# First S5 layer of a four-layer trunk: GpSimd's operator work in tied groups, zeros and counts moved, fewer unread products, another order for sines and tanh

## The chip, the cores and the metric

The kernel runs on one core of one Trainium2 chip. The metric is the device time of one execution in microseconds, lower is better. Before the change it is 2245.62 us (median of three runs, 2242.55 to 2246.93). A core has five engines that work side by side, each in the order of its own queue: PE (TensorE, matmul), VectorE (DVE), ScalarE (ACT), GpSimd (POOL) and SyncE (SP, which here only starts transfers). They wait for each other through semaphores.

## The reference, cut to what matters

The model is a trunk of four layers on 512 tokens of width 1024; layers 0 and 3 mix with S5, layer 1 with gated linear attention, layer 2 with differential attention, and each is followed by a gated feed-forward block. The change touches the first S5 layer (layer 0). There 64 groups of 16 channels each have a diagonal complex state of 64 entries:

```python
dt = jnp.exp(log_dt)[:, None]
ab_mag, ab_ang = jnp.exp(lr * dt), li * dt              # the pole of each state
bb_re = f_re[..., None] * br - f_im[..., None] * bi     # input operator, f from the pole
bb_im = f_re[..., None] * bi + f_im[..., None] * br
# s[t] = ab * s[t-1] + bb @ u[t]   (complex), by an associative scan
y = einsum('bcgp,ghp->bcgh', s_re, cr) - einsum('bcgp,ghp->bcgh', s_im, ci)
z = gelu(y + d_skip * h)
a, b = split(z @ w_glu)                                 # 1024 x 2048 weights
mix = a * sigmoid(b)
```

## The kernel before, in words

Four successive tokens form one step of the scan, so a scan has 128 steps. The 64 groups are 32 pairs on the 128 partitions, and the pairs are worked off in eight blocks of four (`kk` = 0 to 7), each 512 columns wide. For every block the kernel needs operators: `X` (input, with powers 0 to 3 of the pole) and `Q` (output, powers 0 to 4). These are made for two blocks at once, for `h` = 0 to 3, by `cross` (L1228), which multiplies by the powers and adds: three elementwise operations a time (L1239, L1240, L1241). `s5_x` (L1255) gives `X` and three functions: `pre` (the gain, and power 0), `one` (real part of powers 1 to 3) and `two` (imaginary part). `X[0]` is made on VectorE, `X[1]`, `X[2]` and `X[3]` on GpSimd, all of `Q` on VectorE.

The rotation of each state is taken out of the scan, so that the scan runs on real decays (`r4`, L1221), and the phases come from `s5_phases_first` (L1187): PE multiplies `counts` (numbers 0 to 127 on block-selecting rows) with the phase rows `frow`; ScalarE rounds twice ("rough"); PE subtracts ("angle"); VectorE clips; ScalarE takes two sines.

`s5_first` (L1763) sets all this up, and `s5_pipe` (L1542) runs the iterations `kk` = 0 to 9. In iteration `kk`, in this order: `states(kk)` on VectorE (L1593 to L1598; the first four read PE's products `V` from PSUM, the last two have both inputs in SBUF), `outputs(kk - 1)` on PE (`y`, L1628 and L1630) with the gelu on ScalarE (L1632), `up(kk + 2)` and `products(kk + 1)` (V), `turned(kk - 1)` (PE `zp`, ScalarE `zT`), two scans (L1602) and four turn products (L1615, L1611) on VectorE, `rest(kk - 1)` on VectorE (L1653, reads PSUM), and matmuls of the following projection (`glu`, L1666). Hooks of `s5_first` insert operators, phases and transfers at named places. From L1675 (`hand_all`) on, the order on every engine is the program's order; ahead of it a scheduler picks the order, within the limits that `issue_after` sets.

Other pieces that the steps touch:
- The maps `mops` (input to output within a step) go through DRAM: `s5_map` (L1355) adds on VectorE, copies on ScalarE, stores on SP's queue and loads with eight DMAs, four on SP's and four on GpSimd's queue.
- `rps` (L1352) are products of `Q` with the padded `B` (`bp`); PE has them at the start of iterations 2, 4 and 6.
- `zero_off` (L1316) writes zeros into the off-diagonal halves of operator tiles, on ScalarE by copies of zeros out of the identity.
- `warmed(12)` (L1338) is twelve fp32 products of the identity with itself that nobody reads; in the trace they are 24 matmuls.
- Small PSUM tiles are taken in turn from two banks (`tp`), so PE's next transpose waits for the copy of the last but one.
- `s5_glu` (L2022) follows: tanh of four accumulators (`gate`, L2034), which frees their banks, and the product with the other half of the weights, whose tiles are cast on ScalarE (L420) and whose low parts are made on VectorE (L428).

## Time and profile before

| | |
|---|---|
| median of three runs | 2245.62 us |
| the profiled execution's own time | 2241.62 us |
| its span | 2239.9 us |
| TensorE's granted clock, mean | 0.998 |
| busy: PE, VectorE, ScalarE, GpSimd | 97%, 73%, 51%, 15% |
| first S5 layer up to its last `glu` matmul | 0 to 143.9 us |

The profile is one execution recorded by the hardware. A row of a timeline gives the start, the duration, the engine, the line of the kernel, the operation with its output and inputs and their shapes, and how many were merged (x4). What stands in square brackets is how long the engine had been idle before it and what ended that. Neighbouring instructions on one engine overlap a little, so durations add up to more than the elapsed time; the distance from start to start is what counts. The granted clock (PEclk) is 1.00 at full speed and 0.50 at half.

### The profile page before, as it was taken

Reading aid. Unit: us, or ns where it says so; the run is one execution under the profiler, and the core shown is the slowest. Engines: PE = TensorE matmul, PEld = TensorE weight load, DVE = VectorE, ACT = ScalarE, POOL = GpSimd, SP = SyncE. Lnnn points to the kernel's source line nnn. Section 1 sums busy time; section 2 is a strip of 40 time slices with the busy share of each in tenths; the row PEclk is TensorE's granted clock in tenths of the full one; section 3 lists DMA queues with packets and bytes.
Section 4 is the critical chain, followed back from the end, with each engine's and each line's share of the span. In section 5 each row is a group of like instructions: output and inputs, shape, how many; then the busy total and the mean of one; then the engine's idle time right before and its main releaser. Section 6 shows DMA issues by size and latency. Waiting matters only on the chain.

```text
span 2239.9 us, 38438 instructions
## 1 busy us (share of the span) xinstructions
PE 2171.3 (97%) x15415; PEld 1967.9 (88%) x15415; DVE 1635.7 (73%) x2495; ACT 1137.5 (51%) x1827; POOL 337.6 (15%) x447
## 2 busy tenths in 40 slices
PE   6999999999999999999999999999999999999998
PEld 5888979999988899999988888999999888989997
DVE  9965878786877598776745676977766965957675
ACT  8534635444655365564435676644544334635343
POOL 5301141431211010100002221101000001101000
PEclk9999999999999999999999999999999999999999
DMA  4256666774863667765337465985632646766632
GB/s 90 62 175 168 159 167 174 175 183 129 206 158 95 169 162 198 180 170 141 104 128 155 100 151 139 231 223 132 180 95 56 161 142 158 191 166 166 165 76 75
DMA packets 309180, 333.62 MB, mean 149 GB/s; under 512 B 70477, under 2 KB 253033, under 8 KB 308874
## 3 DMA queue, kind: packets, MB, share of 16 engines
q1 hardware_dynamic: 238970, 238.93, 35.3%
q0 software_dynamic: 70032, 92.23, 22.2%
q8 instruction: 121, 1.98, 0.4%
q14 instruction: 57, 0.47, 0.1%
HBM read 297.16 MB, written 18.75 MB: 141 GB/s over the span
## 4 chain that ended last, share of the span: by engine, by line
PE 80%; DVE 10%; ACT 4%; issue 3%; DMA 1%; SPq 1%; POOL 0%; DVEq 0%; POOLq 0%; ACTq 0%
PE a L594 20%; PE acc L448 11%; PE acc L450 11%; PE acc L449 11%; PE c L594 10%; PE d L594 5%; DVE whl L428 2%; PE y L1630 2%; PE acc L1666 2%; ACT whl L420 1%; PE op L2607 1%; PE s L2574 1%; PE tp L117 1%; PE V L1588 1%; PE acc L2662 1%
## 5 line engine op out<-in xcount | busy, mean ns | idle before, releaser
L428 DVE TENSOR_TENSOR whl<-wst,whl 128x1024 fp32r<-128x1024 f32 x260 | 317.0, 1224 | 220.7 <-ACT whl L420 219.7
L594 PE MATMUL a<-side,whl 128*128 128x256 f32 x3240 | 391.8, 277 | 6.6 <-DVE whl L428 6.3
L420 ACT CAST whl<-wst 128x1024 fp32r<-128x1024 f32 x260 | 272.0, 1051 | 244.9 <-PE acc L450 155.8
L594 PEld LDWEIGHTS a<-side,whl 128*128 128x128 f32 x3240 | 378.3, 188 | 8.9 <-DVE whl L428 7.4
L448 PE MATMUL acc<-whl,act 128*128 128x512 f32 x704 | 276.1, 392 | 1.6 <-DVE g L768 1.6
L449 PE MATMUL acc<-whl,act 128*128 128x512 f32 x704 | 274.6, 390 | 0.0
L450 PE MATMUL acc<-whl,act 128*128 128x512 f32 x704 | 274.5, 390 | 0.0
L594 PE MATMUL c<-side,whl 128*128 128x256 f32 x2160 | 260.9, 277 | 3.8 <-DVE whl L428 3.8
L594 PEld LDWEIGHTS c<-side,whl 128*128 128x128 f32 x2160 | 252.6, 188 | 4.7 <-DVE whl L428 4.6
L428 DVE TENSOR_TENSOR whl<-slot,whl 128x1024 fp32r<-128x1024 f32 x105 | 127.8, 1222 | 60.6 <-ACT whl L420 60.5
L448 PEld LDWEIGHTS acc<-whl,act 128*128 128x128 f32 x704 | 132.2, 188 | 30.1 <-DVE g L768 2.2
L450 PEld LDWEIGHTS acc<-whl,act 128*128 128x128 f32 x704 | 132.2, 188 | 27.7
L449 PEld LDWEIGHTS acc<-whl,act 128*128 128x128 f32 x704 | 132.3, 188 | 26.2
L420 ACT CAST whl<-slot 128x1024 fp32r<-128x1024 f32 x105 | 109.9, 1052 | 86.3 <-PE acc L450 46.3
L594 PE MATMUL d<-sides,whl 128*128 128x256 f32 x1080 | 132.3, 278 | 2.5 <-ACT whl L420 2.5
L594 PE MATMUL a<-sides,whl 128*128 128x256 f32 x1080 | 132.4, 279 | 1.9 <-DVE whl L428 1.2
L594 PEld LDWEIGHTS d<-sides,whl 128*128 128x128 f32 x1080 | 127.9, 188 | 3.3 <-ACT whl L420 3.3
L594 PEld LDWEIGHTS a<-sides,whl 128*128 128x128 f32 x1080 | 128.0, 188 | 3.2 <-DVE whl L428 1.4
L428 DVE TENSOR_TENSOR whl<-halves,whl 128x1024 fp32r<-128x1024 f32 x87 | 105.9, 1222 | 31.8 <-ACT whl L420 31.6
L420 ACT CAST whl<-halves 128x1024 fp32r<-128x1024 f32 x87 | 91.0, 1052 | 71.5 <-DVE halves L817 27.2
L759 POOL DMA_DIRECT2D wst<-in_ffn_w_gate_up_dram x44 | 57.1, 1299 | 449.2 <-DMA wst<-in_ffn_w_gate_up_dram 174.0
L865 ACT CAST act<-r 128x512 fp32r<-128x512 f32 (+1 forms) x110 | 66.1, 643 | 106.9 <-DVE r L846 85.7
(506 smaller groups left out, 4039.1 us busy)
## 6 DMA issues: line engine op xcount, KB each, us to landing
wst<-in_ffn_w_gate_up_dram SPq DMA_DIRECT2D x88, 512.0 KB, 4.7
wst<-in_ffn_w_down_dram SPq DMA_DIRECT2D x88, 512.0 KB, 4.6
slot<-in_ffn_w_gate_up_dram SPq DMA_DIRECT2D x69, 512.0 KB, 6.6
wst<-in_ffn_w_gate_up_dram POOLq DMA_DIRECT2D x44, 512.0 KB, 6.1
halves<-in_ffn_w_gate_up_dram SPq DMA_DIRECT2D x42, 512.0 KB, 7.0
wst<-in_s_w_glu_dram SPq DMA_DIRECT2D x32, 512.0 KB, 5.0
wst<-in_diff_w_qkv_dram SPq DMA_DIRECT2D x24, 512.0 KB, 4.3
slot<-in_ffn_w_gate_up_dram POOLq DMA_DIRECT2D x18, 512.0 KB, 9.4
```

The source lines that it names most:

```text
L117: tr.nc.tensor.transpose(p[:, j], h[:, j * P : (j + 1) * P], tr.ident[:])
L420: self.last["high"] = self.nc.scalar.copy(hl[:, 0], w[:])
L428: self.last["low"] = self.nc.vector.tensor_tensor(hl[:, 1], w[:], hl[:, 0].bitcast(F32), op=ALU.subtract)
L448: mm(out, lh, rh, start=first, stop=False)
L449: mm(out, lh, rl, start=False, stop=False)
L450: self.last["mm"] = mm(out, ll, rh, start=False, stop=last)
L594: mm(o, *two, start=first and not (j or k or n), stop=k == 3 and n == 2, skip_group_check=True,)
L759: nc.gpsimd.dma_start(w[:], left.quarter(*plus, b), accum_op=ALU.add)
L865: self.last["act high"] = nc.scalar.copy(dst[:, 0, j], src[:, j])
L1588: mm(V[kk][z][:, bs(b)], inm[:, z, bs(b)], U[:, bs(b)], start=True, stop=True)
L1630: mm(yb[:, b], q[:, j, b], om[:, j // 2, bs(b)], start=False, stop=j == 3)
L1666: mm(accs[t][:], zT[:, m // 2, kk, t * P : (t + 1) * P], hl[:, m % 2, kk % 2], start=kk == 0 and m == 0, stop=kk == KT - 1 and m == 2,)
```

## The change

- **Counts**: eight scaled copies on ScalarE instead of two products on VectorE.
- **Decays**: the copy on ScalarE leaves out the first column of each block; that column is zeroed once per buffer (`s5_no_decay`), in the first S5 on VectorE ahead of everything, in the second S5 (three buffers) on GpSimd. Before, GpSimd zeroed it after every copy.
- **Zeros of the maps**: `mops[0]` on VectorE ahead of everything, `mops[1]` on ScalarE at the end of iteration 0; before, both on ScalarE at the start.
- **Unread products**: `warmed(5)` instead of `warmed(12)`.
- **Sines**: ahead of the loop, clip and sines of block 0 come before the rough step of block 1.
- **GpSimd's X**: `pre`, `one` and `two` no longer run in one go. A group can begin with a copy of one column from a VectorE result into a place of `X` that `two` overwrites later, so that GpSimd waits for that result. `X[1]` (pre, one) waits for the end of `Q[0]`, and its `two` for the second turn product of iteration 0; `X[2]` (pre, one) waits for the end of `Q[1]`, `two` for the second turn product of iteration 2; `X[3]` (pre) waits for the end of `Q[2]`, its `one` and `two` for the second turn product of iteration 4. Before, `X[1]` began after the fourth root of the norm, and `X[2]` and `X[3]` stood at the turns of iterations 1 and 3 without such a wait.
- **Tanh**: in the first half of the first S5's gated projection, casts and low parts from the second weight block on are ordered behind the last tanh and the last low part before them.

```diff
@@ -1162,10 +1162,8 @@
         v.tensor_tensor(sel[:], self.ident[:, 4:8], self.ident[:, 8:12], op=ALU.add)
         self.counts = cp.tile([P, 2, 4, P], F32R, name="counts")
         for z, y in enumerate((self.ident[:, 0:4], sel[:])):
-            v.tensor_tensor(
-                self.counts[:, z], y.unsqueeze(2).broadcast_to([P, 4, P]),
-                self.mrow[:].unsqueeze(1).broadcast_to([P, 4, P]), op=ALU.mult,
-            )
+            for j in range(4):
+                nc.scalar.mul(self.counts[:, z, j], self.mrow[:], y[:, j : j + 1])
         self.nident = cp.tile([P, P], F32R, name="nident")
         nc.gpsimd.tensor_scalar_mul(self.nident[:], self.ident[:], -1.0)
         self.mmagic = cp.tile([P, 1], F32, name="mmagic")
@@ -1222,8 +1220,11 @@
         r = r4.rearrange("p (b m) -> p b m", m=P)
         c = L * NB + 4 * kk
-        self.nc.scalar.copy(r, self.k5["r4"][:, c : c + 4].unsqueeze(2).broadcast_to([P, 4, P]))
-        self.nc.gpsimd.memset(r[:, :, 0:1], 0.0)
+        self.nc.scalar.copy(r[:, :, 1:], self.k5["r4"][:, c : c + 4].unsqueeze(2).broadcast_to([P, 4, P - 1]))
+
+    def s5_no_decay(self, r4, eng):
+
+        eng.memset(r4.rearrange("p (b m) -> p b m", m=P)[:, :, 0:1], 0.0)
     def cross(self, eng, pool, L, b0, nb, s0, ns, out, a, b, op, w):
@@ -1553,6 +1554,7 @@
             q = self.wp.tile([P, 4, 4, P], F32, tag="whl", name="prods", bufs=5)
             nc.gpsimd.memset(q[:, :, :, 0:1], 0.0)
             hold.append((m, q))
+        self.turned_out = lambda kk: hold[kk % 2][1][:, 1, 3, 127:]
         wg = self.i["s5_w_glu"][L]
         stage, hls = {}, {}
         accs = []
@@ -1767,12 +1769,17 @@
         zT = zpool.tile([P, 2, KT, SEQ], F32R, name="zT")
         self.edge(zpool, 32)
         with self.tc.tile_pool(name="s5_0", bufs=1) as p:
+            r4 = {}
             scr, more = (self.hp.tile([P, 4096], F32, tag="hT", name=f"scr{z}") for z in range(2))
             oms = [more[:, 1024 * z : 1024 * z + 1024].rearrange("p (a b) -> p a b", a=2) for z in range(2)]
             mops = [more[:, 2048 + 1024 * z : 3072 + 1024 * z] for z in range(2)]
             bp = p.tile([P, 2, 256], F32, name="bpad")
             rs = p.tile([P, 2, 112], F32, name="rsb")
             inm = [p.tile([P, 2, 512], F32, name=f"inm{z}") for z in range(2)]
+            self.zero_off(mops[0].unsqueeze(1), 64)
+            for n in range(2):
+                r4[n] = p.tile([P, 512], F32, tag="r4", name="r4", bufs=2)
+                self.s5_no_decay(r4[n][:], nc.vector)
             self.s5_small(p)
             for t in range(NT):
                 nc.sync.dma_start(xin[:, t], i["x"][0].rearrange("(p t) c -> p t c", t=NT)[:, t])
@@ -1783,35 +1790,35 @@
                 nc.sync.dma_start(gain[g * 64 : (g + 1) * 64], src[g].partition_broadcast(64))
             raw = {0: self.s5_loads(p, 0, 0, 8, 2)}
             raw[1] = self.s5_loads(p, 0, 8, 8, 2)
-            X, Q, ph, r4 = {}, {}, {}, {}
-
-            def new_x(h):
-                X[h] = self.s5_x(nc.gpsimd if h else nc.vector, p, 0, 8 * h, 8, raw[h][0], 2, gain)
-                for f in X[h][1:] if h else X[h][1:2]:
-                    f()
+            X, Q, ph = {}, {}, {}
+
+            def new_x(h, *parts, behind=None):
+
+                if 0 in parts:
+                    X[h] = self.s5_x(nc.gpsimd if h else nc.vector, p, 0, 8 * h, 8, raw[h][0], 2, gain)
+                if behind is not None:
+                    nc.gpsimd.tensor_copy(X[h][0][:, 1, 7, 3, 15:], behind)
+                for n in parts:
+                    X[h][1 + n]()
             def new_q(h):
                 Q[h] = self.s5_q(nc.vector, p, 0, 8 * h, 8, 2)
                 Q[h][1](self.s5_qt(raw[h][1]))
-            rounded, *rows = self.s5_rows_of_phases(p)
-            for y in inm:
+            for y in inm + oms:
                 self.zero_off(y, 64, nc.scalar)
             self.zero_off(bp[:], 16, nc.scalar)
             nc.gpsimd.memset(rs[:, :, :48], 0.0)
-            for z in range(2):
-                self.zero_off(oms[z], 64, nc.scalar)
-                self.zero_off(mops[z].unsqueeze(1), 64, nc.scalar)
+            rounded, *rows = self.s5_rows_of_phases(p)
             with self.tc.issue_after(self.last_power.ins):
-                new_x(0)
-                X[0][2]()
+                new_x(0, 0, 1)
             self.hand(mybir.EngineType.PE, mybir.EngineType.Activation)
             with self.tc.issue_after(self.last_sine.ins):
                 ps = self.s5_qt(raw[0][1])
-                self.warmed(12)
+                self.warmed(5)
                 hu = self.s5_in(scr, xin, (rounded, rows[0]))
             with self.tc.issue_after(self.last_row.ins):
-                X[0][3]()
+                new_x(0, 2)
                 self.s5_b_pads(bp, X[0][0])
                 Q[0] = self.s5_q(nc.vector, p, 0, 0, 8, 2)
                 Q[0][1](ps, nc.vector)
@@ -1825,7 +1832,7 @@
             def get(kk, name):
                 return {
-                    "in": lambda: inm[kk % 2], "cs": lambda: cs(kk), "r4": lambda: r4[kk][:], "out": lambda: oms[kk % 2],
+                    "in": lambda: inm[kk % 2], "cs": lambda: cs(kk), "r4": lambda: r4[kk % 2][:], "out": lambda: oms[kk % 2],
                     "map": lambda: mops[kk // 2 % 2][:, (kk % 2) * 512 : (kk % 2 + 1) * 512],
                 }[name]()
@@ -1836,8 +1843,7 @@
                     ph[kk][name]()
             def decays(kk):
-                r4[kk] = p.tile([P, 512], F32, tag="r4", name="r4", bufs=2)
-                self.s5_decays(0, kk, r4[kk][:])
+                self.s5_decays(0, kk, r4[kk % 2][:])
             def ins(kk):
                 self.s5_inms(inm[kk % 2], self.s5_xts(X[kk // 2][0], 4 * (kk % 2)))
@@ -1849,10 +1855,7 @@
                 phases((0, "rough"))
                 up(0)
                 ins(0)
-                phases((0, "angle"), (1, "rough"))
-                with self.tc.issue_after(self.last_pow.ins):
-                    new_x(1)
-                phases((0, "clip"), (0, "sines"))
+                phases((0, "angle"), (0, "clip"), (0, "sines"), (1, "rough"))
                 products(0)
                 rows[1]()
                 decays(0)
@@ -1864,6 +1867,10 @@
                 out_pads(0)
                 out_pads(1)
                 raw[2] = self.s5_loads(p, 0, 16, 8, 2)
+                new_x(1, 0, 1, behind=behind_q(0))
+
+            def behind_q(h):
+                return Q[h][0][:, 1, 7, 4, 15:]
             def first(kk):
                 if kk == 2:
@@ -1894,8 +1901,10 @@
                     self.s5_map(0, 8 * h, 8, rv[h], rs, mops[h % 2])
             def ahead_of_rest(kk):
-                if kk in (1, 3):
-                    new_x(kk // 2 + 2)
+                if kk in (0, 2):
+                    new_x(kk // 2 + 1, 2, behind=self.turned_out(kk))
+                if kk == 4:
+                    new_x(3, 1, 2, behind=self.turned_out(kk))
             def ahead_of_zp(kk):
                 if kk == 0:
@@ -1935,8 +1944,13 @@
                     out_pads(kk + 1)
             def last(kk):
+                if kk == 0:
+                    self.zero_off(mops[1].unsqueeze(1), 64, nc.scalar)
                 if kk == 1:
                     phases((4, "clip"), (5, "clip"))
+                    new_x(2, 0, 1, behind=behind_q(1))
+                if kk == 3:
+                    new_x(3, 0, behind=behind_q(2))
             rv = {}
             hooks = {
@@ -2001,6 +2015,8 @@
                 left.finish()
                 up(0)
                 products(0)
+                for y in css:
+                    self.s5_no_decay(y[:, 2], nc.gpsimd)
                 for kk in range(2):
                     decays(kk)
                 up(1)
@@ -2031,7 +2047,7 @@
                 def evac_b(t, ps):
                     gate[t] = p.tile([P, 512], F32, tag="gate", name="gate", bufs=6)
-                    nc.scalar.activation(gate[t][:], ps[:], AF.Tanh, scale=0.5)
+                    self.last["gate"] = nc.scalar.activation(gate[t][:], ps[:], AF.Tanh, scale=0.5)
                 def evac_a(t, ps):
                     v.scalar_tensor_tensor(gate[t][:], gate[t][:], 1.0, ps[:], op0=ALU.add, op1=ALU.mult)
@@ -2047,7 +2063,9 @@
                     self.gemm_b(stat, wg, KT, D + d * 512, evac_b)
                 ahead = (lambda: (nxt.ahead(2), nxt.total("3"))) if d else None
                 with nullcontext() if d else self.tc.issue_after(self.last_turned.ins):
-                    self.gemm_b(stat, wg, KT, d * 512, evac_a, tail=4 if d else 0, ahead=ahead)
+                    behind = None if d or L else {"silu": self.last.pop("gate"), "scaled": self.last["low"]}
+                    self.gemm_b(stat, wg, KT, d * 512, evac_a, tail=4 if d else 0, ahead=ahead, behind=behind)
+            self.last.pop("gate")
         return nxt
```

## The prediction

> **What bounds the kernel now.** I read the page first, then the windows of the first 150 us, then the timelines of single engines there. Over the whole span PE is the bound:
>
> ```profile
> span 2239.9 us, 38438 instructions
> PE 2171.3 (97%) x15415; PEld 1967.9 (88%) x15415; DVE 1635.7 (73%) x2495; ACT 1137.5 (51%) x1827; POOL 337.6 (15%) x447
> ```
>
> Only some 69 us are without a matmul. Many lie in the first S5 layer, as its windows show (columns: length, busy us of PE, PEld, DVE, ACT, POOL, granted clock, DMA):
>
> ```profile
> 40.00:50.00 10.00, 9.25 (x99) 7.94 (x97) 10.00 (x15) 9.78 (x18) 5.14 (x8) 1.00 0.44 94
> 50.00:60.00 10.00, 6.02 (x63) 5.00 (x64) 9.93 (x13) 7.05 (x12) 9.69 (x11) 0.92 0.10 21
> ```
>
> VectorE is full and PE is not; where PE idles most (50 to 60), POOL is full too. ScalarE is nearly full from 40 to 50: whoever takes VectorE off the path meets ScalarE next. From 100 us on PE is full but for one gap at 143.9. So a microsecond saved on PE's own order before 144 us should arrive at the end, and one saved on another engine only as far as PE was waiting for it.
>
> The next rows show the price of POOL beside VectorE (start, duration, engine, line; what an instruction costs is the time from its start to the next one's):
>
> ```profile
> 44.14 0.68 DVE L1597 TENSOR_TENSOR mods<-mods 128x512 f32<-128x512 f32 x1
> 33.12 0.68 DVE L1596 TENSOR_TENSOR mods<-V,cs 128x512 f32<-128x512 f32 x1
> 33.72 1.41 DVE L1597 TENSOR_TENSOR mods<-mods 128x512 f32<-128x512 f32 x1
> ```
> ```profile
> 32.64 0.84 POOL L1240 TENSOR_TENSOR dx<-X,pw 128x384 f32<-128x384 f32 x1
> ```
>
> With POOL quiet the sum of two SBUF tiles (44.14) takes 0.68, and operations follow each other by 0.60. With POOL at work one that reads PSUM (33.12, the next at 33.72) still costs 0.60, and POOL's own beside it 0.84; the same sum of SBUF tiles (33.72) takes 1.41. That is what the tie to PSUM reads is to avoid. [...]
>
> **Part 1, the start (until the first states).** These rows carry it:
>
> ```profile
> 17.03 1.98 PE L1285 MATMUL cps<-ident,craw 128*64 128x128 f32 x16 [11.63 <-DMA craw<-in_s_c_re_dram]
> 18.93 3.83 PE L1342 MATMUL warmed<-ident 128*128 128x128 f32 x24
> 22.60 0.60 PE L1182 MATMUL frow<-ident,params 128*12 128x128 f32 x4
> 24.77 0.66 ACT L1201 ACTIVATE turns<-rough,magic 128x512 f32<-128x512 f32 x1
> 26.70 1.17 ACT L1409 COPY inm<-xps 64x512 f32<-64x512 f32 x2
> 28.05 0.69 ACT L1201 ACTIVATE turns<-rough,magic 128x512 f32<-128x512 f32 x1 [0.18 <-PE rough L1200]
> 29.40 0.61 ACT L1215 ACTIVATE cs<-cs 128x512 f32<-128x512 f32 x1
> ```
> ```profile
> 7.40 0.68 DVE L1165 TENSOR_TENSOR counts<-ident,mrow 128x512 fp32r<-128x512 f32 x1
> 31.32 0.69 DVE L1593 TENSOR_TENSOR mods<-V,cs 128x512 f32<-128x512 f32 x1 [0.31 <-ACT cs L1217]
> 5.53 5.01 ACT L1322 COPY scr<-ident 64x512 f32<-64x512 f32 x8
> 2.92 0.22 DVE L1059 COPY params<-params 64x128 f32<-64x128 f32 x1 [1.86 <-DMA params<-in_s_log_dt_dram]
> ```
>
> Two products for the counts (0.6 each) leave VectorE, which works without a break there, so the phase parameters come 1.2 earlier. PE gets no earlier than its data (17.03). The unread products fall from 24 matmuls to 10; in the trace the first run at about 0.21 and the later ones at 0.11 apart, so ten end near 21.0, and the frow transposes start 1.5 earlier; their inputs come 1.2 earlier, and had waited for PE. The first turns go from 24.77 to about 23.25. Then the order: sines of block 0 now stand ahead of the rough step of block 1 (28.05 to 29.40, 1.35). The copies inm end at 26.3, the clip on VectorE at about 26.5, the sines at 28.4, the V products (2.0 after inm) at 28.4: the states start at 28.5 instead of 31.32, **2.8 earlier**. VectorE is in time: it loses 1.2 of counts, and with X of the second group gone from POOL until Q is done its X and Q operations are no longer stretched.
>
> The zeros: eight copies of 0.62 become two on VectorE in its 1.86 of idle ahead of 2.92 (at most 1.25, by the copies' row), four stay, and two go to the end of iteration 0 on ScalarE. ScalarE's counts are eight 128-wide operations; no row has them. The nearest, the 64x128 ones at 45.30 below, give about 0.28, so 2.2; the 512-wide copies bound them by 0.62, so 5.0; below zero is excluded, since they are added. I take 2.2: ScalarE then is free at about 10.2, ahead of the sine.
>
> **Part 2, iterations 0 and 1: ScalarE takes over.**
>
> ```profile
> 31.20 0.56 ACT L1183 CAST frow<-frow 12x512 fp32r<-12x512 f32 x1
> 45.30 1.11 ACT L1306 ACTIVATE Q<-cps 64x128 f32<-64x128 f32 x4
> 50.18 0.60 ACT L1632 ACTIVATE gain<-y 128x512 f32<-128x512 f32 x1
> ```
> ```profile
> 34.98 0.69 ACT L1201 ACTIVATE turns<-rough,magic 128x512 f32<-128x512 f32 x1 [0.80 <-PE rough L1200]
> ```
> ```profile
> 41.75 0.68 DVE L1593 TENSOR_TENSOR mods<-V,cs 128x512 f32<-128x512 f32 x1
> 58.16 0.68 DVE L1653 TENSOR_TENSOR zT<-zp,zT 128x512 fp32r<-128x512 f32 x1
> 99.95 0.68 DVE L1593 TENSOR_TENSOR mods<-V,cs 128x512 f32<-128x512 f32 x1
> 112.17 0.69 DVE L1653 TENSOR_TENSOR zT<-zp,zT 128x512 fp32r<-128x512 f32 x1
> ```
> ```profile
> 50.83 0.66 PE L1567 MATMUL up<-ident,scr 128*128 128x128 f32 x4 [1.58 <-ACT gain L1632]
> 54.92 0.39 PE L1200 MATMUL rough<-counts,frow 128*128 128x512 f32 x1
> 58.29 1.10 PE L1352 MATMUL rps<-Q,bpad 128*32 128x64 f32 x30 [2.75 <-DVE Q L1241]
> 64.15 1.06 PE L1630 MATMUL y<-scr,prods 128*128 128x128 f32 x8
> 88.46 0.68 PE L1352 MATMUL rps<-Q,bpad 128*32 128x64 f32 x30 [1.16 <-DVE Q L1241]
> ```
>
> ScalarE's list from the frow cast to the gelu is 19.0 long and holds 1.2 of waits (0.80 the largest), so 17.8 of work. It now begins at 29.75 (sines 28.4, then the moved rough step 1.35), has the two zero copies more (1.25) and, by its own inputs, about 0.8 of waits (turns of block 2 wait for PE's xps, rps and angle in their two banks). Gelu: 29.75 + 17.8 + 1.25 + 0.8 = 49.6, only 0.6 earlier. V of block 2 and the rough steps on PE follow: their end goes from 55.3 to 54.7. Next in PE's order stands rps, which waited for Q until 58.29. VectorE now starts the second states at 39.1 (end of their sines), and from there to Q's end took 16.4 (41.75 to 58.16). The same list without POOL beside it took 12.2 (99.95 to 112.17), with one clip more 12.8, so 3.6 was POOL's X[2]. Q ends at 51.9, at 53.5 if X[1]'s last part costs two meetings. So rps doesn't wait: it ends at 55.4, y of block 1 (4.5 at full clock) at 59.95 instead of 65.2: **5.25 earlier** on PE.
>
> The waits that are added stand on POOL. Behind the one on Q[0] stand the four DMA issues of the map, which wait for their data until about 37 in any case, since SP sends that behind the pads of Q; behind them the second part of X[1], done by 42.5 and read by xps at 45; X[2] starts at Q[1]'s end, into VectorE's wait and its PSUM reads; X[3] ends near 95 and is read near 100. SP's pads of B wait for X as before. Each has microseconds to spare, so I count none. POOL's zeros for the decays (0.1 each) held nobody up; so in the second S5, where three replace eight.
>
> **Part 3, the second wait for Q.**
>
> ```profile
> 73.30 0.68 DVE L1593 TENSOR_TENSOR mods<-V,cs 128x512 f32<-128x512 f32 x1
> 88.33 0.68 DVE L1653 TENSOR_TENSOR zT<-zp,zT 128x512 fp32r<-128x512 f32 x1
> ```
>
> At 88.46 PE waited 1.16 more (with the broken-off pair before it 1.4 in all). From its states to Q's end VectorE took 15.0 there (73.30 to 88.33) against the quiet 12.2, so 2.8 on meetings with X[3]; without them Q is done first. **1.4**.
>
> **Part 4, the tanh.**
>
> ```profile
> 139.10 4.81 PE L1666 MATMUL acc<-whl,zT 128*128 128x512 f32 x20
> 143.86 1.04 ACT L420 CAST whl<-wst 128x1024 fp32r<-128x1024 f32 x1 [2.00 <-DMA wst<-in_s_w_glu_dram]
> 145.45 0.50 PE L448 MATMUL acc<-whl,zT 128*128 128x512 f32 x1 [1.54 <-ACT gate L2034]
> ```
>
> A cast that waits for its weights stands ahead of the four tanh, and PE needs the bank of the first. With the casts of the second block on behind the tanh, the first can run when its bank is complete (near 142), and PE goes on: **1.5**. The second block's cast moves to about 144.5 (less the gain), ahead of PE's need by the 5.5 that 24 matmuls of the first block take.
>
> **The sum**: 5.25 + 1.4 + 1.5 = 8.15. One thing speaks against it, a new hole in PE: in the replay xps of block 2 ends at 46.4 and PE waits for gelu until 49.7 or 50.1, over 3 us where it was 1.58. What an idle of that size does, the windows show:
>
> ```profile
> 59.00:60.00 1.00, 1.00 (x17) 0.83 (x9) 1.00 (x3) 0.13 (x1) 0.92 (x2) 0.50 0.31 65
> 61.00:62.00 1.00, 1.00 (x7) 1.00 (x7) 1.00 (x3) 0.00 (x0) 0.00 (x0) 0.61 0.87 89
> ```
>
> After 2.75 of idle the granted clock fell to 0.50 and came back between 61 and 62, some 3.4 later, which costs 1.7. In the new hole it would fall on V of block 2, which everything waits for. So I subtract 1.7: **6.45**. [...]
>
> The profiled execution took 2241.6 (span 2239.9); it becomes 2235.2. The median of the runs shown is 4.0 above it, 2245.6, and the forecast goes by that: **2239.1**.
>
> **Rivals.**
> *No new slow clock*: 8.15, time 2237.5. Chance 0.22; forecast with it 0.36.
> *VectorE was the only bound*, ScalarE's list having more air than I read: 2.8 at the start, 0.7 (33.72) and 3.6 of meetings, then 1.4 and 1.5 make 10, or 2235.6. ScalarE at 9.78 of 10 speaks against it. 0.03.
> *ScalarE hides it*: the counts cost 5.0 instead of 2.2, or the clip comes behind more of Q, and ScalarE's list begins 2 later. Part 2 shrinks to 3.25, less 1.7 for the clock: 4.45, or 2241.2; 3 later still gives 3.45. Within 0.2% (about 4.5 us, what a measurement of this kernel can tell from no change). For it: ScalarE has no slack after 28 us. 0.33.
> *Slower, the cold start*: with ten unread products PE's clock stays at half through the first iteration. Doubling each PE step on the chain (frow, xps, angle, V, again frow to rough) puts ScalarE's turns of block 2 from 34.98 to 42.1, gelu to 58.4, PE's y of block 1 to 3.5 later than before; less 1.4 and 1.5 that is 0.6 slower. If half speed lasts through y of block 0 (4.5 more, and gelu waits for it), 5.1 slower: 2250.7. It decides if the clock is not up by about 30 us. Against it: in the trace products sped up after 3.7 us of unbroken work, and 10 products with the transposes still give over 4. 0.06.
>
> Faster by over 0.2%: 0.36 + 0.22 + 0.03 = 0.61; within: 0.33 and a part of the last, 0.34; slower 0.05. The range runs from nearly no gain (0.6) to the whole relief (10): 2235.5 to 2245.
>
> **What would show it.** Right: counts as eight ACT rows ahead of the sine; states at about 28.5; VectorE's Q at 0.6 each; no PE wait before rps; two ACT copies behind Q's at 44; PE's wait ahead of up at about 50, followed by a clock of 0.5 or not; tanh before the second cast and PE unbroken at about 137. Wrong: Q still at 1.3, frow later than 21.5, gelu after 51, a clock of half at 25 to 40.

## The result, and the profile after

| | before | after |
|---|---|---|
| median, same chip, 11 runs each | 2243.18 us (2242.42 to 2247.68) | 2239.89 us (2237.25 to 2242.55) |
| span of the profiled execution | 2239.9 us | 2236.7 us |
| first matmul of the gated projection (L448) | 145.45 us | 141.09 us |
| gelu of block 0 | 50.18 us | 51.30 us |

The ratio is 0.998, with a 95% interval of 0.9971 to 0.9989: between 2.5 and 6.5 us faster. The two medians differ by 3.3. The forecast was 6.45 faster, at the far edge of that interval and about twice the difference of the medians. The time of 2239.1 lies so near to 2239.89 partly because the three runs that it started from had a median 2.4 above the eleven here.

The whole gain is there by the gated projection, 4.36 earlier. These are the head of the page of the changed kernel, and the second of the two windows that stood at the head of the prediction:

```profile
span 2236.7 us, 38395 instructions
...
PE 2171.9 (97%) x15401; PEld 1969.6 (88%) x15401; DVE 1629.1 (73%) x2497; ACT 1139.5 (51%) x1833; POOL 329.0 (15%) x440
```
```profile
50.00:60.00 10.00, 8.05 (x65) 7.12 (x66) 6.13 (x11) 5.70 (x9) 5.07 (x11) 0.66 0.30 48
```

From 50 to 60 VectorE fell from 9.93 to 6.13: it is no longer what PE waits for. PE's 8.05 busy is no gain by itself, because its granted clock fell from 0.92 to 0.66. PE's timeline of the changed kernel shows both (start, duration, engine, line, tiles, idle time ahead and its releaser):

```profile
31.66 1.15 PE L1387 MATMUL xps<-ident,X 64*64 64x64 f32 x32 [2.43 <-ACT frow L1181]
...
51.95 1.12 PE L1569 MATMUL up<-ident,scr 128*128 128x128 f32 x4 [2.85 <-ACT gain L1634]
53.01 3.78 PE L1590 MATMUL V<-room,inm 128*128 128x128 f32 x16
...
58.73 0.69 PE L1353 MATMUL rps<-Q,bpad 128*32 128x64 f32 x32
...
136.43 4.81 PE L1668 MATMUL acc<-whl,zT 128*128 128x512 f32 x20
141.09 0.39 PE L448 MATMUL acc<-whl,zT 128*128 128x512 f32 x1
```

`rps` no longer waits for `Q` (2.75 before), and the projection no longer waits for the tanh (1.54 before). But `up` starts 1.12 later than before, after a longer idle, and V behind it takes 3.78 where it took 2.05. In windows of half a microsecond the granted clock is 0.50 from about 51.2 to 58.0, for 6.8 us; behind the wait for `Q` before, it was 0.50 from about 58.4 to 61.8, for 3.4. ScalarE's list shows why `up` is late:

```profile
25.08 1.18 ACT L1410 COPY inm<-xps 64x512 f32<-64x512 f32 x2
27.78 0.63 ACT L1213 ACTIVATE cs<-cs 128x512 f32<-128x512 f32 x1 [1.52 <-DVE cs L1210]
...
31.05 0.56 ACT L1181 CAST frow<-frow 12x512 fp32r<-12x512 f32 x1
...
46.30 1.25 ACT L1323 COPY scr<-ident 64x512 f32<-64x512 f32 x2
...
51.30 0.60 ACT L1634 ACTIVATE gain<-y 128x512 f32<-128x512 f32 x1
```

The frow cast comes at 31.05, and came at 31.20 before: of the earlier start 0.15 is left here. The same list of 17.8, the same 1.2 of waits, and the two copies of zeros (1.25, at 46.30) follow: 31.05 + 17.8 + 1.2 + 1.25 = 51.3.

On VectorE the clip of block 0 stands behind operations of `Q`, and the states of block 0 follow the sines:

```profile
26.33 0.69 DVE L1241 TENSOR_TENSOR dq<-Q,pw 128x512 f32<-128x512 f32 x1
27.05 0.69 DVE L1210 TENSOR_SCALAR cs<-angle 128x512 f32<-128x512 f32 x1
...
29.71 0.69 DVE L1595 TENSOR_TENSOR mods<-V,cs 128x512 f32<-128x512 f32 x1 [1.37 <-ACT cs L1215]
...
53.80 0.69 DVE L1242 TENSOR_TENSOR Q<-Q,dq 128x512 f32<-128x512 f32 x1
58.30 0.69 DVE L1655 TENSOR_TENSOR zT<-zp,zT 128x512 fp32r<-128x512 f32 x1 [3.80 <-ACT zT L1651]
```

The states start 1.6 earlier (31.32 before). `Q` of the second pair of blocks ends at 54.5 instead of 58.2, and then VectorE idles for 3.80. GpSimd's second group stands just there:

```profile
54.62 0.18 POOL L1800 COPY X<-Q 128x1 f32<-128x1 f32 x1 [9.75 <-DVE Q L1242]
...
58.07 0.84 POOL L1240 TENSOR_TENSOR X<-X,pw 128x384 f32<-128x384 f32 x1
```

What comes behind the projection moved with it up to the second S5 layer. PE's rows at its entry, before and then after:

```profile
1737.44 1.91 PE L1567 MATMUL up<-ident,hu 128*128 128x128 f32 x16
...
1744.59 2.26 PE L1588 MATMUL V<-room,operators 128*128 128x128 f32 x16 [0.65 <-POOL cs L1226]
...
1756.03 1.95 PE L1588 MATMUL V<-room,operators 128*128 128x128 f32 x16
```
```profile
1732.38 1.91 PE L1569 MATMUL up<-ident,hu 128*128 128x128 f32 x16
...
1737.47 4.71 PE L1590 MATMUL V<-room,operators 128*128 128x128 f32 x24 [1.13 <-DMA cs<-cs]
...
1752.58 1.95 PE L1590 MATMUL V<-room,operators 128*128 128x128 f32 x16
```

The changed kernel arrives 5.06 earlier (1737.44 against 1732.38), although it had a stretch of half clock near 640 that the kernel before didn't have, and is 3.45 ahead at 1752.58. It has a stretch of half clock more here: from 1736 to 1740 the mean granted clock was 1.00 before and is 0.67 now. Other profiled executions of these kernels have such stretches near 640, 1740 and 1755, some of them and some not, 3.4 us at 0.50 or twice that, so 1.7 us of lost time each or 3.4. From the projection to the end the thirteen traces of this document took between 2094 and 2101 us, the kernel before the least. Executions of one kernel lie 4 to 10 us apart, so the experiments are read by the profiled start of the projection, which lies ahead of these stretches, together with the ratio of many runs. One execution of e11 below took 4409.69 us, which no trace explains, and its ratio leaves it out.

### The profile page after: what moved, and what is told of

Same layout as the page of the kernel before. It is cut to its first block, busy times and chain, and to the rows that moved or that the text cites. A ratio compares the mean times of both kernels' runs of the same rounds, so it can differ in the third digit from the quotient of the medians.

```text
span 2236.7 us, 38395 instructions
## 1 busy us (share of the span) xinstructions
PE 2171.9 (97%) x15401; PEld 1969.6 (88%) x15401; DVE 1629.1 (73%) x2497; ACT 1139.5 (51%) x1833; POOL 329.0 (15%) x440
## 4 chain that ended last, share of the span: by engine, by line
PE 82%; DVE 9%; ACT 4%; issue 3%; DMA 1%; POOL 0%; SPq 0%; DVEq 0%; POOLq 0%; ACTq 0%
PE a L594 20%; PE acc L448 11%; PE acc L450 11%; PE acc L449 11%; PE c L594 10%; PE d L594 5%; DVE whl L428 2%; PE y L1632 2%; PE acc L1668 2%; ACT whl L420 1%; PE V L1590 1%; PE op L2625 1%; PE s L2592 1%; PE tp L117 1%; PE acc L2680 1%
## 5 line engine op out<-in xcount | busy, mean ns | idle before, releaser
L448 PE MATMUL acc<-whl,act 128*128 128x512 f32 x704 | 276.0, 392 | 1.4 <-DVE g L768 1.4
L448 PEld LDWEIGHTS acc<-whl,act 128*128 128x128 f32 x704 | 132.2, 188 | 29.7 <-DVE g L768 1.8
L449 PEld LDWEIGHTS acc<-whl,act 128*128 128x128 f32 x704 | 132.2, 188 | 26.3
```

The costliest lines, as they stand in the source:

```text
L448: mm(out, lh, rh, start=first, stop=False)
L449: mm(out, lh, rl, start=False, stop=False)
```

## The experiments

My theory after the result and the first of these runs: GpSimd's groups in their new places, tied, and the tanh bring the gain; the earlier start is spent in ScalarE's list; and the hole ahead of `up` costs a clock that could be kept. The rivals: the start brings a good part and the ties little; and the clock is of no weight.

The time up to the projection falls into three parts: up to the gelu of block 0 (L1632 or L1634 on ScalarE, which `up` of block 2 waits for); from the start of that `up` to `rps`, which is 4.41 at full clock (50.83 to 55.24 in the kernel before), and longer where the clock falls; and the rest, worked out as the start of the projection less the gelu's start less what "up to rps" has above 4.41. The ratio is to the kernel before, on the same chip; the medians of different rows come from different chips and don't compare. The table's first four columns are of one trace each.

| run | gelu | up to rps | projection | rest | median | ratio, 95% interval |
|---|---|---|---|---|---|---|
| before | 50.18 | 4.41 | 145.45 | 95.27 | 2243.18 | |
| after | 51.30 | 6.78 | 141.09 | 87.42 | 2239.89 | 0.9980 (0.9971 to 0.9989) |
| e1 zeros by GpSimd at the start | 52.16 | 4.40 | 140.26 | 88.11 | 2239.19 | 0.9977 (0.9969 to 0.9986) |
| e2 products in the hole | 51.33 | 4.40 | 138.82 | 87.50 | 2242.04 | 0.9983 (0.9974 to 0.9992) |
| e3 clip first | 50.37 | 5.79 | 139.20 | 87.45 | 2240.70 | 0.9986 (0.9976 to 0.9996) |
| e4 before, tanh alone | 50.09 | 4.42 | 143.58 | 93.48 | 2243.72 | 0.9993 (0.9984 to 1.0002) |
| e5 later zeros by GpSimd, clip first | 49.87 | 6.03 | 138.91 | 87.42 | 2238.14 | 0.9976 (0.9967 to 0.9985) |
| e6 groups alone | 50.15 | 5.93 | 140.75 | 89.08 | 2242.57 | 0.9996 (0.9986 to 1.0006) |
| e7 no ties | 56.53 | 6.92 | 146.47 | 87.43 | 2244.62 | 1.0000 (0.9991 to 1.0009) |
| e8 twelve products at the start | 52.24 | 5.33 | 140.60 | 87.44 | 2241.55 | 0.9988 (0.9979 to 0.9997) |
| e9 e5 with 24 products in the hole | 49.78 | 3.68 | 138.79 | 89.74 | 2240.93 | 0.9981 (0.9972 to 0.9989) |
| e10 groups and tanh | 50.77 | 6.05 | 139.94 | 87.53 | 2240.84 | 0.9987 (0.9978 to 0.9996) |
| e11 e5 with 12 products in the hole | 49.80 | 4.41 | 137.31 | 87.51 | 2238.70 | 0.9975 (0.9964 to 0.9985) |

The ten kernels with the groups in their new places and the tanh edit (after, e1 to e3, e5, e7 to e11) have a rest of 87.4 to 87.5, whatever else was edited, but for e1 and e9, where PE waited further on for a copy of `rps` by ScalarE (0.51 and 0.40) and in e9 for the products as well. So behind the gelu it is almost only PE's own order that counts; what decides is when ScalarE comes to the gelu and whether PE's clock holds behind it. Between before and after the rest fell by 7.85, the gelu came 1.12 later and the clock took 2.37: together the 4.36.

### The parts alone

**e6**: the changed kernel with only the groups of `X`, their ties and the decays' zeros; counts, maps' zeros, products at the start, order of the sines and tanh are those of before.

```diff
-            for j in range(4):
-                nc.scalar.mul(self.counts[:, z, j], self.mrow[:], y[:, j : j + 1])
+            v.tensor_tensor(self.counts[:, z], ...)
...
-                phases((0, "angle"), (0, "clip"), (0, "sines"), (1, "rough"))
+                phases((0, "angle"), (1, "rough"), (0, "clip"), (0, "sines"))
```

> Of the change only GpSimd's X in tied groups and the decays' zeros once; counts, zeros of the maps, 24 unread matmuls, order of the sines and the tanh as in the kernel before. Theory (the ties take VectorE off the path, the other edits of the start cancel each other on ScalarE): Q's operations at 0.6, states at about 31, gelu at about 50.2, no wait of PE for Q, rps end at about 56 instead of 59.4 and no half clock there; the tanh wait of 1.5 stays; the first matmul of the gated projection at 139.5 to 140.5 against 145.45 before and 141.1 with the whole change. Rival (the gain is from the start's edits): 143 or later.

Measured, on PE:

```profile
51.86 3.58 PE L1592 MATMUL V<-room,inm 128*128 128x128 f32 x16 [0.40 <-ACT inm L1412]
...
56.73 0.69 PE L1355 MATMUL rps<-Q,bpad 128*32 128x64 f32 x32
...
140.75 0.50 PE L448 MATMUL acc<-whl,zT 128*128 128x512 f32 x1 [1.45 <-ACT gate L2052]
```

With the gelu where it was before (50.15), `rps` doesn't wait, and the projection starts 4.70 earlier than before although the clock took 1.52 from V. The regrouped `X` with its ties, alone, brings as much as the whole change, and 6.2 in the rest. The ratio of this run (0.9996) shows less of it than the trace: its interval reaches to 3.1 us and doesn't take in the 4.70. What is missing is not accounted for: from the projection to the end the profiled execution took 2100.05, and the one of the kernel before 2094.45; it has a stretch of half clock from 645 to 649 that the one before doesn't have, 1.7 of these 5.6, and no trace shows whether the others have it.

**e4**: the kernel before with the tanh edit alone.

```diff
+                    behind = None if d or L else {"silu": self.last.pop("gate"), "scaled": self.last["low"]}
-                    self.gemm_b(stat, wg, KT, d * 512, evac_a, tail=4 if d else 0, ahead=ahead)
+                    self.gemm_b(stat, wg, KT, d * 512, evac_a, tail=4 if d else 0, ahead=ahead, behind=behind)
```

> The kernel before, with the one edit that orders the casts of the second weight block and later behind the last tanh. Theory: the 1.54 us that PE waited for the first tanh go away and nothing else changes: the first matmul of the gated projection at 143.9 instead of 145.45, the end 1.5 us earlier (0.07%, under what five rounds can tell, so the trace decides). Rival: the later cast delays PE at its second weight block, and the gain comes back as a wait near 149.

Measured, on PE:

```profile
58.27 1.10 PE L1352 MATMUL rps<-Q,bpad 128*32 128x64 f32 x30 [2.81 <-DVE Q L1241]
...
143.58 0.39 PE L448 MATMUL acc<-whl,zT 128*128 128x512 f32 x1
```

The wait for `Q` stands as it was, and the projection starts without a wait, 1.87 earlier (1.8 in the rest): the 1.54 of the wait and small differences ahead of it. The interval of the ratio takes in no change, so only the trace shows this part. The two parts add up: 6.19 in e6 and 1.79 here are 7.98, and the rest of the whole change is 7.85 less.

**e10**: e6 with e4's edit; that is, the changed kernel with the start as before.

> The changed kernel with the start as before (counts by VectorE, zeros of the maps all at the start, 24 unread products, rough step of block 1 ahead of the sines of block 0), with the tied groups, the decays' zeros and the tanh. If the start's edits bring nothing in the end: the first matmul of the gated projection 1.5 ahead of the 140.75 of e6, at 139.2, median as the changed kernel's or up to 1.5 below it. Rival (the start's 1.6 arrives): milestone later than the changed kernel's 141.1 by 1 or more once the clock's losses are taken out, median 2241 or more.

The projection starts at 139.94, 1.15 earlier than with the start's edits, and not the 1.5 ahead of e6 that was expected, because this execution's gelu came 0.6 later than e6's (frow at 23.18 instead of 22.58, behind the same 24 unread products, which took 4.55 instead of 3.98). Even so its gelu is 0.53 earlier than the changed kernel's, the clock took 0.73 less, and the rest is the same. So the edits at the start, all together, bring nothing to the projection in these traces; they put it back by 0.5 to 1.2. The two ratios (0.9987 and 0.998) cannot be told apart.

**e7**: the changed kernel without the waiting copies.

```diff
-                if behind is not None:
-                    nc.gpsimd.tensor_copy(X[h][0][:, 1, 7, 3, 15:], behind)
```

> The changed kernel without GpSimd's waiting copies; the groups stay at their places in GpSimd's order. Theory (the ties matter where a group would run beside Q or the scans): X[1] starts near 22 beside X[0] and Q[0] and pushes the clip and the sines about 1.3 later; X[2]'s first group runs from 45 beside the scan, the turns and Q[1], Q[1] ends 2 to 3 later, near 57, still ahead of rps at 58.7; the projection's first matmul 1 to 1.5 later than 141.1. Rival (places alone do it): no difference at the projection.

The loss was 5.4, and not where I expected it. GpSimd, and what waited for it on ScalarE:

```profile
19.30 1.03 POOL L1265 TENSOR_TENSOR bb<-bb,gain 128x256 f32<-128x256 f32 x1 [5.18 <-DVE dx L1241]
20.31 0.59 POOL L541 TENSOR_TENSOR rs<-ms,mhalf 128x1 f32<-128x1 f32 x1
```
```profile
20.93 1.15 ACT L1528 ACTIVATE scr<-xin,rs 128x1024 f32<-128x1024 f32 x1 [3.80 <-POOL rs L541]
```

Without the copy the scheduler put the first group ahead of GpSimd's small powers for the norm (L541); ScalarE stood for 3.80, frow came at 23.02 instead of 20.73, and the states started at 33.47 instead of 29.71. From the states to the gelu it took 1.5 more, with PE at half clock on the way (0.50 from 37 to 39), and there is the gelu at 56.53, 5.2 later. The rest is that of the changed kernel. VectorE's operations on `Q`, 0.69 each in the changed kernel, were stretched beside GpSimd's (26.97, and 60.07 twice over):

```profile
26.97 0.89 DVE L1241 TENSOR_TENSOR dq<-Q,pw 128x512 f32<-128x512 f32 x1
...
60.07 1.49 DVE L1240 TENSOR_TENSOR Q<-Q,pw 128x512 f32<-128x512 f32 x1
...
62.20 0.69 DVE L1242 TENSOR_TENSOR Q<-Q,dq 128x512 f32<-128x512 f32 x1
```

The second `Q` ended at 62.9, and `rps` stood at 64.10: late gelu and half clock hid what VectorE lost. At full clock `rps` would have come 4.41 behind `up`'s 57.18, at 61.6, and have waited 1.3. So e7 shows that the ties also keep an order, and gives 1.3 (an estimate from these rows) for what they save on VectorE at the second `Q`; how much of e6's 6.2 comes from the copies that wait and how much from the groups' later places in the program is not told apart by these runs.

### The start

**e8**: 24 unread matmuls instead of ten (`warmed(12)` at the start). **e3**: the last operations of `Q[0]` behind the clip of block 0:

```diff
-                Q[0][3]()
...
-                phases((0, "angle"), (0, "clip"), (0, "sines"), (1, "rough"))
+                phases((0, "angle"), (0, "clip"))
+                Q[0][3]()
+                phases((0, "sines"), (1, "rough"))
```

> The changed kernel with 24 unread matmuls at the start again instead of 10. Theory (the clip waited for VectorE's Q, ScalarE idle 1.5 ahead of the sines, so the earlier frow was hidden): frow at 22.3 instead of 20.7, clip at 27.2 to 27.5 instead of 27.05, the rest 0.2 to 0.5 later. Rival (the path runs through PE's frow): all 1.5 later, the projection at 142.6. If the ten had not sufficed for the clock, this one would show faster matmuls from 21 to 26, which the changed kernel's trace doesn't ask for.

> The changed kernel, with the second half of Q[0] (three VectorE operations, 1.9 us) moved from ahead of the first clip to behind it. Theory (the start gained only 1.6 of 2.8 us because the clip stood behind these): clip at 25.9 instead of 27.05, first states at 28.7 instead of 29.7, first gelu at about 50.3 instead of 51.3, the projection's first matmul 1 us earlier, 140.1. Rival (the start is hidden, since ScalarE meets waits of its own behind it): states 1 us earlier, gelu as before at 51.3, no gain.

VectorE in e3:

```profile
26.09 0.69 DVE L1210 TENSOR_SCALAR cs<-angle 128x512 f32<-128x512 f32 x1 [0.21 <-PE angle L1207]
...
28.76 0.69 DVE L1595 TENSOR_TENSOR mods<-V,cs 128x512 f32<-128x512 f32 x1
```

In e8 the states started at 30.64 and the gelu came at 52.24, 0.93 and 0.94 later: fewer products are worth that much here. The size is this trace's: its 24 products took 4.42, and in the other four traces that have them at the start 3.77 to 4.55. Its projection starts 0.5 earlier all the same, because the clock took 0.92 instead of 2.37. In e3 the clip waited for nothing but PE; states and gelu came 0.95 and 0.93 earlier. That is the missing part of the start: it was queued behind `Q`.

**e1**: the zeros of the second map by GpSimd at the start; **e5**: the same by GpSimd ahead of `up(0)`, with e3's order.

```diff
+                self.zero_off(mops[1].unsqueeze(1), 64, nc.gpsimd)
...
             def last(kk):
-                if kk == 0:
-                    self.zero_off(mops[1].unsqueeze(1), 64, nc.scalar)
```

> The changed kernel, with the zeros of the second maps written by GpSimd near the start instead of by ScalarE at the end of iteration 0. Theory (ScalarE's list from the first sines to the first gelu sets the pace there): the list is 1.25 us shorter, the first gelu goes from 51.3 to about 50.05 and the first matmul of the gated projection from 141.1 to 139.9; if the shorter hole in PE also spares the half clock on V of block 2, to about 138.2. Against the kernel before 5.6 to 7.3 us faster, not 4.4. Rival (PE's clock alone decides, or VectorE does): gelu earlier, the projection's first matmul unchanged at 141.

> The changed kernel with two repairs: the zeros of the second maps on GpSimd (behind the roots of the norm, where it idles) instead of at the end of iteration 0 on ScalarE, and the clip of block 0 ahead of the second half of Q[0]. Theory (ScalarE's list up to the first gelu sets the pace): first states at 28.7, gelu at 49.1 (51.3 less 1.25 less 1.0), hole in PE ahead of up 1.6, clock full on V of block 2, the first matmul of the gated projection at 136.5 (141.1 less 2.25 less the half clock's 1.7 and some in up and zp), 137.5 to 138.5 if a slow window falls into PE's other hole near 30. Rival (VectorE's Q[1] or PE's own work bounds by now): gelu at 49.1, but the projection not below 138.

In e1 the hole ahead of `up` shrank as the theory said and V kept its clock, but the gelu came later, not earlier. First PE, then VectorE and GpSimd at the start of e1:

```profile
32.33 1.69 PE L1387 MATMUL xps<-ident,X 64*64 64x64 f32 x32 [2.29 <-ACT frow L1181]
...
52.81 0.66 PE L1569 MATMUL up<-ident,scr 128*128 128x128 f32 x4 [1.60 <-ACT gain L1634]
53.86 2.05 PE L1590 MATMUL V<-room,inm 128*128 128x128 f32 x16 [0.40 <-ACT inm L1410]
```
```profile
4.92 0.89 DVE L1000 TENSOR_SCALAR params<-params 128x64 f32<-128x64 f32 x1
```
```profile
4.82 0.95 POOL L1160 MEMSET frow<- 128x1024 f32 x1
```

Two things took the gain: a memset that now ran beside VectorE's first parameters made one of them 0.89 long instead of 0.21, and the half clock fell into the other hole, the one of 2.29 ahead of `xps`, which the moved sines had opened. In e5 that hole is 1.40 and the clock holds there: the gelu comes at 49.87 and the projection at 138.91, behind the 136.5 to 138.5 expected. Of the miss, 0.77 is again GpSimd's zeros. They did not run behind the roots of the norm, as was meant, but at 5.39, beside VectorE's parameters (0.68 where the changed kernel has 0.20 for the same operation), and the clip came at 26.86, 0.77 later than in e3:

```profile
5.28 0.68 DVE L1001 TENSOR_SCALAR params<-params 128x64 f32<-128x64 f32 x1
```
```profile
5.39 0.52 POOL L1326 MEMSET scr<- 64x512 f32 x1
```

Against that start, the gelu is 1.27 earlier than in e3, which is the price of the two copies on ScalarE. Another 1.62 was lost to the clock behind `up`.

### The clock in the hole

**e2**: the changed kernel with 24 matmuls that nobody reads between the second inputs and `up` of block 2. **e9**: the same in e5. **e11**: e9 with 12 matmuls.

```diff
                 if 1 <= kk < 7:
                     ins(kk + 1)
+                if kk == 1:
+                    self.warmed(12)
```

> The changed kernel, with 24 unread matmuls of the identity on PE between xps of block 2 and the wait for the first gelu, which fill most of the hole of 2.85 us. Theory (the idle hole lets PE's clock fall to half, and V of block 2 pays): granted clock 1.00 from 52 to 57, V of block 2 takes 2.05 instead of 3.78, and the first matmul of the gated projection goes from 141.1 to about 139.1 (V 1.7, up and zp some 0.7, less what the rest was waiting for anyway). Rival (the slow V was hidden behind other work): clock back at 1.00, but the projection's first matmul stays at 141.

> The kernel of e5 (zeros of the second map by GpSimd, clip ahead of the rest of Q) with 24 unread matmuls behind the second inputs, as in e2. If the clock in the hole is what is left: granted clock 1.00 from 45 to 60, V of block 2 takes 2.05 instead of 2.97, the first matmul of the gated projection near 137.2 instead of 138.9, and the median some 1.5 below e5's, near 2236.6. Rival (the products stand ahead of up and hold PE): up later than 50.5, milestone 138.9 or later. A window at 285, 640 or 1740 that comes or goes may still move a single execution by 1.7 to 3.4.

> The kernel of e9 with 12 unread matmuls in the hole instead of 24. They end near 50.2, ahead of the gelu's end at 50.4, so they hold nothing. If half a hole is enough to keep the clock: up at 50.5, V at 2.0, the first matmul of the gated projection near 137.3 (e5 138.9, e9 138.8), median 1 to 1.5 below e5's and e9's where the later windows fall alike. Rival (what is left of idle, about 0.3 and the waits around it, still takes the clock): V near 3, milestone 138.8.

PE in e2, e9 and e11:

```profile
49.05 2.94 PE L1343 MATMUL warmed<-ident 128*128 128x128 f32 x24
51.98 0.66 PE L1569 MATMUL up<-ident,scr 128*128 128x128 f32 x4
53.03 2.05 PE L1590 MATMUL V<-room,inm 128*128 128x128 f32 x16 [0.40 <-ACT inm L1410]
```
```profile
48.77 2.94 PE L1343 MATMUL warmed<-ident 128*128 128x128 f32 x24
51.55 0.60 PE L1569 MATMUL up<-ident,scr 128*128 128x128 f32 x4
```
```profile
48.79 1.60 PE L1343 MATMUL warmed<-ident 128*128 128x128 f32 x12
50.45 0.66 PE L1569 MATMUL up<-ident,scr 128*128 128x128 f32 x4
51.51 2.05 PE L1590 MATMUL V<-room,inm 128*128 128x128 f32 x16 [0.40 <-ACT inm L1410]
...
137.31 0.39 PE L448 MATMUL acc<-whl,zT 128*128 128x512 f32 x1
```

e2 differs from the changed kernel in nothing but these products, `up` starts at the same time, V is back at 2.05, and the projection starts 2.27 earlier: that is what the half clock cost. In e9 the same 24 are too many, because the gelu is earlier: they end at 51.55, `up` could have started at 50.4, and what the clock gives they take away, with waits further on (138.79 against e5's 138.91). Twelve end in time, and the projection starts at 137.31, 8.1 ahead of before and 3.8 ahead of the changed kernel. The median of e2 doesn't show its 2.27, and e11's ratio of 0.9975 overlaps that of the changed kernel: e11 and e5 beat the kernel before, but that they beat the changed one is shown by the trace alone.

## Why the prediction held, point by point

The direction and the mechanism were right; the size was not. Of the 6.45 forecast, 4.36 is there at the projection: 1.70 went with the later gelu, 0.67 with the longer half clock, and 0.28 came on top in the rest.

**The bound**: right as far as this pair shows it. 4.36 at the projection became 3.2 in the span, the difference lost to one more stretch of half clock in the second S5. That every microsecond ahead of the projection arrives at the end isn't shown: e6 has 4.70 there and little in its ratio.

**Part 1, the start**: the mechanism was right, the size was not. Counts as eight rows of ScalarE cost 0.29 to 0.34 each:

```profile
8.26 1.28 ACT L1166 ACTIVATE counts<-mrow,ident 128x128 fp32r<-128x128 f32 x4
9.44 0.68 ACT L1166 ACTIVATE counts<-mrow,params 128x128 fp32r<-128x128 f32 x2
```

0.28 was expected. Six ran ahead of the sine and two behind it, and ScalarE had them done in time. The first turns came at 23.15 (23.25 expected), the copies inm ended at 26.3 as said. Then the step failed that reads "the clip on VectorE at about 26.5, the sines at 28.4": I let the clip start when `angle` was ready, and it stood in VectorE's queue behind `Q`. It ended at 27.7, so 1.6 was gained instead of 2.8; e3 gives back 0.95 of the 1.2.

**Part 2**: "5.25 earlier", less 1.7 for the clock, became 1.1: `up` of block 3, behind `y` of block 1, starts at 66.49 instead of 67.61. "ScalarE takes over" was right, and so were its list of 17.8 and its 1.25 of zeros. The step that failed is "29.75 + 17.8 + 1.25 + 0.8 = 49.6": the list begins at 31.05, because of the clip, and holds 1.2 of waits, so the gelu is 1.7 later than forecast, and "gelu after 51", one of the forecast's signs of being wrong, came with 51.30. That the hole would take the clock on V was right too, but its 1.7 was 2.37: it was worked out from one stretch of 3.4 us, and the clock stayed at 0.50 for twice that. In the three parts of the table the forecast was 0.58 less for the gelu, 1.7 more for the clock and 7.57 less for the rest; measured were 1.12 more, 2.37 more and 7.85 less. Most of the miss is ScalarE's start. `Q` ended at 54.5, later than the 51.9 to 53.5 forecast, and nothing on PE waited for it. The two meetings in that 53.5 were my estimate, at 0.8 each (1.41 at 33.72 less 0.60); here the last operation of `X[1]` (1.35, at 43.52) ran beside two sums on VectorE, of 0.75 (43.24) and 1.50 (43.91).

The contention came out as the rows had said: GpSimd's 384-wide operations took 0.84 beside PSUM reads and 1.30 to 1.35 beside sums of SBUF tiles, and VectorE's last sums 1.17, 1.33 and once 1.50 instead of 0.68. The stretched operations lay where VectorE was not the bound.

**Part 3**: "1.4" was right. No wait stands before `rps` of the third pair of blocks (88.46 before, after a wait of 1.16); of the 2.6 between them, 1.1 is Part 2's:

```profile
85.84 0.69 PE L1353 MATMUL rps<-Q,bpad 128*32 128x64 f32 x32
```

**Part 4**: "1.5" was right: PE goes from the last `glu` matmuls to L448 without a break. e4 shows it alone.

**Decays**: "held nobody up; so in the second S5" was wrong by 0.65. In the kernel before PE waited that long at 1744.59 for GpSimd's zeros; the wait is gone, and half clock took its place.

**The rivals**: "ScalarE hides it" is nearest to what happened, 4.45 for a list that starts 2 later; it started 1.3 later, with more waits and a costlier clock, and 4.36 was left. "No new slow clock" falls with V at 3.78, and "VectorE was the only bound" with VectorE's idle 3.80 at 58.30. The cold start didn't come: the first V, at 26.31, took 2.05, as V did at full clock, and the granted clock was 1.00 from 20 to 40.

## What to carry to other kernels

Read the price of a second elementwise engine per neighbour: beside PSUM reads it was free here (0.60 from start to start, at 33.12 before), beside sums of SBUF tiles it doubled them (1.41 against 0.68), and a one-column copy that waits for the right result kept it in its place (0.18 to 0.20 four times in the changed kernel, 1.17 and 1.00 at 69.28 and 93.93). When a wait is taken off one engine, replay the next engine's list from its true start, what is queued ahead of it included; a hole of 2.85 that this opened on PE cost a slow stretch as well (0.50 for 6.8 us), and unread matmuls, no longer than the hole, bought it back (2.27 at the projection in e2). Work moved to an engine that was full (the zeros on ScalarE, 1.25) was paid in full: without it, in e5, the gelu came 1.27 earlier than in e3, counted from the clip.

## What the runs showed of the hardware beyond that

- The same idle of 2.85 to 2.87 ahead of `up` cost 2.4 to 2.5 in the changed kernel and e7, 1.38 in e3 and 0.92 in e8. In the first two the granted clock was 0.50 for 6.8 us, in e3 and e8 for 3.4. Idle of 1.6 ahead of `up` and 0.40 behind it cost 1.5 to 1.6 in e5, e6 and e10, with 3.4 at 0.50, and nothing in e1, e4 and before. So the length of the idle alone did not set the price here; what else did, these runs do not show.
- One-input VectorE operations took longer beside GpSimd operations that only write, too: 0.89 instead of 0.21 beside a memset of 0.95 in e1, and 0.68 instead of 0.20 beside one of 0.52 in e5. In e9 and e11, with the same start, the clip came as late as in e5 (26.86): at 26.78 and 26.82.
- At the very start the granted clock doesn't show how slow the matmuls are: in the kernel before it is 1.00 from 19 to 21, where five unread products took 1.27 from 19.52 on, while 24 of the same products took 2.94 in e2's hole, half as long each.
